# Another order of the down pairs, a longer delay before the first transposes, and a split tail, in a fused hybrid decoder layer

## The chip, the cores and the metric

The kernel runs on one core of a Trainium2 chip. The metric is the device time of one execution in microseconds. Engines are named as in the profile: PE (matmul), PEld (PE's weight loads), DVE (vector), ACT (scalar), POOL, SP (the engine whose queue issues most transfers).

## The reference

One decoder layer on 272 positions (16 meta tokens and 256 tokens), all float32. What the change touches is the feed-forward part:

```
u = rmsnorm(h, ffn_norm_w)                       # (256, 2048) matter
h = h + (silu(u @ w_gate) * (u @ w_up)) @ w_down # w_gate, w_up: (2048, 5632); w_down: (5632, 2048)
return h[:, LEAD:]                               # (256, 2048)
```

Before it stand the input projection, the attention and delta-rule heads and the output projection. They are the first 500 us or so, and the change leaves them alone.

## The kernel before

**Three matmuls for one product.** A float32 weight tile is loaded as `raw` (128 x 2 x 512, 512 KB, by SP's queue, 4 buffers), then split: ACT casts it to a rounded `hi` (L274), DVE subtracts to get `lo` (L275). Activations are kept in the same two parts. A product of 128x128 by 128x512 is then three matmuls on PE: hi by hi, hi by lo, lo by hi. In the feed-forward part there are 6 buffers for pairs of `hi` and `lo`, so splitting runs at most 6 split tiles ahead of PE.

**Chunks and blocks.** Gate and up run in 11 chunks of 512 hidden columns; the product of silu(gate) and up goes through PE transposes (`to_hT`, L1277) into `hT`, the activations of down. Chunk 0 is written by itself: `ffn_task` multiplies on DVE (L1306) and then transposes. Down runs in two blocks of 1024 output columns, `block(NCH + p, ...)` for p = 0, 1, called block 0 and block 1 here. A block goes over 22 pairs q of two k-tiles, each with two weight tiles (columns 0 to 511 and 512 to 1023 of the block).

**Plain pairs and seven pairs.** A plain pair uses its two tiles in 8 products, which is 24 matmuls. A pair listed in `DSEVEN` (7, 9, 11, 13, 15, 17, 19) is done in 7 products, 21 matmuls, by a Strassen-like scheme: both raw tiles (g, then u) have to be there, DVE forms two tiles of sums `t` and `s` by four instructions (L291 to L294), and four split tiles come of it: g, half of u, t, s. So a seven pair takes 4 of the 6 split buffers where a plain pair takes 2, and it costs DVE more and PE less. It also needs sums of the activations, made once per pair before block 0 gets there (`down_side`, `side_forms`, DVE L1318 to L1330, called side work), and the last three chunks of `hT` have to be split too (`whole`, L1466 and L1468).

**What sets the order.** The Python code is a recorder. Each `tasks.step()` between products lets side tasks emit a little work, and a `yield n` in a task makes it wait n steps. ACT's and SP's instructions stay in the order in which they were emitted; a scheduler orders PE's and DVE's when the kernel is built, and from then on every engine runs its list strictly in order. `next_w` emits the splits of tiles up to 6 ahead of the one that PE is given, and raw loads up to 3 ahead of that.

**The tail.** When a half of a block is complete, `down_end` adds it to the residual on DVE (L1516) and stores it (L1518) through SP's queue. The residual is fetched back from DRAM (`fetch_x1`, L1484) by the same queue; block 1's fetch has to wait until block 0's output has left the buffers. The last half is stored in two pieces per token block.

Of the kernel before, what the change touches and what calls it, by code (L numbers as in the profile page):

```python
# [15 lines left out]
P = 128  # L16
D = 2048
KT = D // P
# [3 lines left out]
FFN = 5632  # L22
# [3 lines left out]
NCH = FFN // 512  # L26
# [5 lines left out]
WR, WS = 4, 4  # L32
WS2 = 2
WHOLE = 8
SEVEN = (2, 4, 6)
DSEVEN = (7, 9, 11, 13, 15, 17, 19)
PER_STEP = 2
# [129 lines left out]
def layer(tc, xT, aw, x, w_in, w_ba, w_out, w_gate, w_up, w_down, cmask, dist, par, out):  # L167
    nc = tc.nc
    V, S, G, PE = nc.vector, nc.scalar, nc.gpsimd, nc.tensor
# [20 lines left out]
    tasks = Tasks(PER_STEP)  # L190
# [29 lines left out]
    wd_v = w_down.rearrange("(kt p) c -> p kt c", p=P)  # L220
    order = []
# [12 lines left out]
    def w_tile(wv, q, c):  # L234
        return wv[:, 2 * q:2 * q + 2, 512 * c:512 * (c + 1)], 2, 512
# [4 lines left out]
    forms = [("w", i) for i in range(len(order))]  # L240
    for c in range(1, NCH):
        for q in range(KT // 2):
            i = len(order)
            order += [w_tile(wv, q, c) for wv in (wg_v, wu_v)]
            forms += [("w", i), ("w", i + 1)] if q not in SEVEN else [("g", i), ("u", i), ("t", i), ("s", i)]
    for c in (0, 2):
        for q in range(FFN // P // 2):
            i = len(order)
            order += [w_tile(wd_v, q, c + j) for j in range(2)]
            forms += [("w", i), ("w", i + 1)] if q not in DSEVEN else [("g", i), ("u", i), ("t", i), ("s", i)]  # L250
    raws, ready, sums_ = {}, {}, {}

    pos = [0, 0, 0, 0]
# [127 lines left out]
    for k in range(KT):  # L381
        src, w = xr[k // 8][:, k % 8, :], aw_sb[:, k:k + 1]
# [889 lines left out]
    def to_hT(c, b, h_):  # L1272
# [7 lines left out]
        if c not in hT:  # L1280
# [3 lines left out]
            elif c < 7:  # L1284
                hT[c] = keep.tile([P, 2, 4, SEQ], F32R, tag=("v_c", "k_c", "q_c")[c - 4], name=n)
            elif c < WHOLE:
                hT[c] = fpool[0].tile([P, 2, 4, SEQ], F32R, tag=n, name=n)
            else:
                hT[c] = fpool[0].tile([P, 4, SEQ], F32, tag=n, name=n)
        bs = slice(P * b, P * (b + 1))  # L1290
        if c < WHOLE:
            S.copy(hT[c][:, 0, :, bs], pst)
# [6 lines left out]
    def ffn_task(c, b, pg, pu):  # L1299
        g_ = yield from fpool[1].get(512)  # L1300
        act(g_, pg, AF.Silu, scale=rr[:, b:b + 1])
        mm.free()
        yield at_least(f"up{c}", 1)
        yield 1
        ps = pu[b]
        V.scalar_tensor_tensor(g_, ps, rr[:, b:b + 1], g_, ALU.mult, ALU.mult)  # L1306
        mm.free()
        yield 2
        yield from to_hT(c, b, g_)


# [52 lines left out]
        yield 10  # L1364
        yield from to_hT(c, b, h_)

    def block(c, name, nq, seven, lhs, need, mid, end):

        ring, other = rings[c % 2], rings[(c + 1) % 2]
        tasks.until(lambda: ring.live == 0)  # L1370
        x = [ring.now() for _ in range(4)]
        y = []
        n = nq - len(seven)
        left = {("x", i): 3 * (2 * n + (len(seven) if i < 3 else 0)) for i in range(4)}
        left.update({("y", i): 3 * len(seven) for i in range(4)})
        todo = dict(left)

        def product(bank, a, w):
            for l, r in ((a[0], w[0]), (a[0], w[1]), (a[1], w[0])):
                first, todo[bank] = todo[bank] == left[bank], todo[bank] - 1  # L1380
                PE.matmul((x if bank[0] == "x" else y)[bank[1]], l, r, start=first, stop=todo[bank] == 0)  # L1381

        for q in range(nq):
            k = 2 * q
            if need:
                tasks.until(need(k))
            if q not in seven:
                for col in range(2):
                    hi, lo = next_w()
                    for i in range(2):  # L1390
                        for b in range(2):
                            product(("x", 2 * col + b), lhs(k + i, b), (hi[:, i], lo[:, i]))
                            tasks.step()
                    if q == nq - 1:
                        end(col, x)
                continue
            if not y:
                tasks.until(lambda: other.live == 0)
                y += [other.now() for _ in range(4)]
            tasks.until(at_least(f"side{(name, q)}", 1))  # L1400
            s1, s2_, s3, s4 = sides[name, q]
            plan = (((("y", 0), lhs(k, 0), 0), (("x", 0), lhs(k + 1, 0), 1)), ((("x", 2), s4, 1),),
                    ((("y", 3), s1, 0), (("y", 2), s3, 1)), ((("y", 1), s2_, 0), (("x", 1), lhs(k + 1, 1), 1)))
            for part in plan:
                hi, lo = next_w()
                for bank, a, i in part:
                    product(bank, a, (hi[:, i], lo[:, i]))
                    tasks.step()
            if q == seven[-1]:
                mid(y)  # L1410

    def chunk(c):
        t = []

        def end(col, x):
            if col == 0:
                for b in range(2):
                    tasks.spawn(end_task(c, b, x, t), urgent=True)

        def mid(y):  # L1420
            tasks.until(lambda: fpool[1].live == 0)
            t.extend(fpool[1].now((512,)) for _ in range(4))
            S.copy(t[0], y[0])
            tasks.spawn(mid_task(c, y, t), delay=0, urgent=True)

        block(c, "u", KT // 2, SEVEN, lhs_u, None, mid, end)
        mark(f"up{c}")

    def keep_x1():
# [16 lines left out]
    for i, q in enumerate(SEVEN):  # L1446
        k = slice(2 * q, 2 * q + 2)
# [7 lines left out]
    def whole(c):  # L1455
# [19 lines left out]
    def fetch_x1(p):  # L1475

        for j in range(2):
            n = f"hT{WHOLE + j}"
            if p == 0:
# [29 lines left out]
    def down_end(p, b, c, ps):  # L1509
        yield at_least("mid_d", p + 1)  # L1510
        parts = 1 if (p, c) != (1, 1) else 2
        w = 512 // parts
        for i in range(parts):
            cs = slice(w * i, w * (i + 1))
            r_ = x1n[p, c][:, b, cs]
            V.tensor_tensor(r_, r_, ps[:, cs], ALU.add)  # L1516
            o = 1024 * p + 512 * c + w * i
            nc.sync.dma_start(out=out[P * b:P * (b + 1), o:o + w], in_=r_)  # L1518
        rings[(NCH + p) % 2].free()

    def down_side(i, q):
# [20 lines left out]
        tasks.spawn(down_side(i, q), delay=24)  # L1542
    tasks.spawn(fetch_x1(0), delay=24)
    for p in range(2):
        def end(col, x):
            for b in range(2):
                tasks.spawn(down_end(p, b, col, x[2 * col + b]), urgent=True)

        def mid(y):
            tasks.until(lambda: fpool[1].live <= 1)  # L1550
            t = [fpool[1].now((512,)) for _ in range(3)]
            S.copy(t[0], y[0])
            tasks.spawn(down_mid(p, y, *t), delay=0, urgent=True)

        block(NCH + p, "h", FFN // P // 2, DSEVEN, lhs_h, need_h, mid, end)
        if p == 0:
            tasks.spawn(fetch_x1(1), delay=12)
    tasks.until(lambda: not tasks.list)
# [66 lines left out]
```

## Time and profile before

| | us |
|---|---|
| median of 3 runs (1222.12 to 1224.43) | 1222.2 |
| profiled execution, own time | 1224.38 |
| profiled execution, span from first to last instruction | 1222.6 |
| PE busy in the span | 1209.2 |
| DVE busy | 983.6 |
| ACT busy | 692.3 |

The clock granted to PE is full (0.9 or more) in all slices of the span. PE is busy 99% of the time, so only what makes PE stand still, and what stands before its first and behind its last matmul, can change the time unless the number of matmuls does. A busy matmul of 512 columns is shown as 0.39 us but a new one starts every 0.227 us; the matmuls overlap.

### The profile page before, as it was taken

The page shows a single profiled execution, that of the slowest core. Times are in us where ns is not written, and L with a number is a line of the kernel's source. Part 1 is how long each engine was busy: PE and PEld are TensorE (multiplying, and loading weights), DVE is VectorE, ACT ScalarE, POOL GpSimd, SP SyncE. Part 2 cuts the span into 40 slices and gives each one's busy share as a digit, 9 for nine tenths or more (in the row PEclk, how much of TensorE's full clock was granted, in tenths as well). Part 3 has the DMA queues.
Part 4 walks back from the last instruction along what each step waited for, and adds up shares of the span by engine and source line. Part 5 has one row for each costly group of instructions (what it writes and reads, how often), then busy time and mean ns, then how long its engine had stood idle before and what let it go on. Part 6 is the DMA issues. An engine that isn't in the chain of part 4 may idle for free.

```text
span 1222.6 us, 19223 instructions
## 1 busy us (share of the span) xinstructions
PE 1209.2 (99%) x7316; PEld 1060.0 (87%) x7316; DVE 983.6 (80%) x1573; ACT 692.3 (57%) x1087; POOL 6.1 (0%) x14
## 2 busy tenths in 40 slices
PE   9999999999999999999999999999999999999998
PEld 7999999999999988887888888888888888888876
DVE  7989974686676666668889988998998899886686
ACT  7674465275776665455555556555555665553552
POOL 0000000000000000000000000000000000000000
PEclk9999999999999999999999999999999999999999
DMA  8466564344544645685665665566566565567543
GB/s 293 124 207 195 145 187 121 112 124 145 172 140 139 229 162 178 191 277 167 196 206 186 195 218 190 192 204 217 166 208 216 187 211 197 201 225 276 181 164 133
DMA packets 151869, 228.54 MB, mean 187 GB/s; under 512 B 11736, under 2 KB 72672, under 8 KB 151264
## 3 DMA queue, kind: packets, MB, share of 16 engines
q1 hardware_dynamic: 151232, 226.78, 57.4%
q8 instruction: 57, 0.93, 0.3%
q10 hardware_dynamic: 544, 0.52, 0.1%
q14 instruction: 36, 0.29, 0.1%
HBM read 221.83 MB, written 5.45 MB: 186 GB/s over the span
## 4 chain that ended last, share of the span: by engine, by line
PE 85%; DVE 7%; DMA 4%; ACT 2%; issue 1%; SPq 0%; DVEq 0%; ACTq 0%
PE aux L1381 25%; PE mm L1152 23%; PE mm L1381 21%; PE mm L1199 10%; DVE lo L275 3%; DMA raw<-in_w_down_dram 3%; ACT hi L274 1%; PE aux L1100 1%; PE aux L1055 1%; DMA raw<-in_w_in_dram 0%; PE mm L1277 0%; DVE s L293 0%; DMA raw<-in_w_up_dram 0%; DVE r L581 0%; PE aux L1277 0%
## 5 line engine op out<-in xcount | busy, mean ns | idle before, releaser
L274 ACT CAST hi<-raw 128x1024 fp32r<-128x1024 f32 (+1 forms) x412 | 405.1, 996 | 325.0 <-PE mm L1152 93.3
L275 DVE TENSOR_TENSOR lo<-raw,hi 128x1024 fp32r<-128x1024 f32 (+1 forms) x412 | 470.6, 1153 | 141.6 <-ACT hi L274 139.1
L1152 PE MATMUL mm<-xh,hi 128*128 128x272 f32 (+2 forms) x896 | 258.4, 289 | 0.0
L1152 PE MATMUL mm<-xl,hi 128*128 128x272 f32 (+2 forms) x896 | 255.9, 286 | 0.9 <-DVE xl L384 0.6
L1152 PE MATMUL mm<-xh,lo 128*128 128x272 f32 (+2 forms) x896 | 255.0, 286 | 1.0 <-DVE lo L275 1.0
L1152 PEld LDWEIGHTS mm<-xl,hi 128*128 128x128 f32 x896 | 168.5, 188 | 2.2 <-DVE xl L384 2.0
L1152 PEld LDWEIGHTS mm<-xh,hi 128*128 128x128 f32 x896 | 168.6, 188 | 2.1 <-issue 1.5
L1152 PEld LDWEIGHTS mm<-xh,lo 128*128 128x128 f32 x896 | 168.2, 188 | 1.6 <-DVE lo L275 1.4
L1381 PE MATMUL aux<-hi,uh 128*128 128x512 f32 x260 | 101.6, 391 | 0.0
L1381 PE MATMUL mm<-hi,uh 128*128 128x512 f32 x260 | 101.6, 391 | 0.0
L1381 PE MATMUL aux<-hi,ul 128*128 128x512 f32 x260 | 101.3, 390 | 0.0
L1381 PE MATMUL mm<-hi,ul 128*128 128x512 f32 x260 | 101.2, 389 | 0.0
L1381 PE MATMUL aux<-lo,uh 128*128 128x512 f32 x260 | 101.2, 389 | 0.0
L1381 PE MATMUL mm<-lo,uh 128*128 128x512 f32 x260 | 101.2, 389 | 0.0
L1381 PE MATMUL aux<-hi,hT 128*128 128x512 f32 x216 | 70.2, 389 | 0.0
L1381 PE MATMUL mm<-hi,hT 128*128 128x512 f32 x216 | 70.0, 389 | 0.0
L274 ACT CAST hi<-s 128x1024 fp32r<-128x1024 f32 x44 | 46.3, 1053 | 38.0 <-DVE s L294 34.5
L291 DVE TENSOR_TENSOR t<-raw,raw 128x512 f32<-128x512 f32 x44 | 30.2, 687 | 38.7 <-DMA raw<-in_w_down_dram 25.2
L274 ACT CAST hi<-t 128x1024 fp32r<-128x1024 f32 x44 | 46.3, 1053 | 26.2 <-DVE t L292 11.3
L1381 PEld LDWEIGHTS aux<-hi,ul 128*128 128x128 f32 x260 | 48.8, 188 | 10.2
L1381 PEld LDWEIGHTS mm<-hi,ul 128*128 128x128 f32 x260 | 48.8, 188 | 10.2
L1381 PEld LDWEIGHTS mm<-hi,uh 128*128 128x128 f32 x260 | 48.8, 188 | 10.0
(418 smaller groups left out, 2046.8 us busy)
## 6 DMA issues: line engine op xcount, KB each, us to landing
raw<-in_w_in_dram SPq DMA_DIRECT2D x111, 512.0 KB, 3.6
raw<-in_w_gate_dram SPq DMA_DIRECT2D x88, 512.0 KB, 3.7
raw<-in_w_up_dram SPq DMA_DIRECT2D x88, 512.0 KB, 4.4
raw<-in_w_down_dram SPq DMA_DIRECT2D x88, 512.0 KB, 4.6
raw<-in_w_out_dram SPq DMA_DIRECT2D x32, 512.0 KB, 4.2
x<-x1d SPq DMA_DIRECT2D x8, 256.0 KB, 4.8
xr<-in_xT_dram SPq DMA_DIRECT2D x7, 272.0 KB, 5.8
out_dram<-x SPq DMA_DIRECT2D x6, 256.0 KB, 5.1
```

What stands on the lines that cost most here:

```text
L274: S.copy(hi[:, js], raw[:, js])
L275: V.tensor_tensor(lo[:, js], raw[:, js], hi[:, js], ALU.subtract)
L291: V.tensor_tensor(t[:, 0], u[:, 0], g[:, 0], ALU.subtract)
L1055: PE.matmul(pss[m][:, cut[n]], q[ms, P * n:P * (n + 1)], k[ms, 0:NK[n]], start=True, stop=True)
L1100: PE.matmul(po[:, n, :], l, r, start=(j == 0), stop=(j == 1 + n))
L1152: PE.matmul(acc[c][:, 0:n], a[:, k, cs], b[:, kt, t0:T], start=(kt == 0 and i == 0), stop=(kt == KT - 1 and i == 2))
L1199: PE.matmul(acc[b], l, r[:, i % 2, :], start=(first and i == 0 and j == 0), stop=(last and i == len(kts) - 1 and j == 2))
L1381: PE.matmul((x if bank[0] == "x" else y)[bank[1]], l, r, start=first, stop=todo[bank] == 0)
```

## The change

Four edits:

- `ROWS` sets, for each block, at which of the 22 positions a seven pair (S) or a plain pair (N) stands. The pairs of each kind keep their order. Before, pairs ran 0 to 21 in both blocks, which is `NNNNNNNSNSNSNSNSNSNSNN`.
- In `ffn_task` (chunk 0) the step count before the transposes goes from 2 to 8.
- In the last tile of block 1 PE does both products of token block 0 first, then both of token block 1 (before: alternating), and `down_end` of token block 0 is emitted between them.
- The second piece of each of the last two stores goes out through ACT's queue instead of SP's.

```
+ROWS = ("NNNNNSNSNNSNSNNSNSNSNN", "NNSNNSNNSNNSNSNSNSNNNN")
...
+    def down_rows(p):
+        plain = iter(q for q in range(FFN // P // 2) if q not in DSETS[p])
+        seven = iter(DSETS[p])
+        return [next(plain if r == "N" else seven) for r in ROWS[p]]
...
         mm.free()
-        yield 2
+        yield 8
         yield from to_hT(c, b, g_)
...
+                    last = c == NCH + 1 and col == 1 and q == rows[-1]
+                    for j in range(4):
+                        i, b = (j % 2, j // 2) if last else (j // 2, j % 2)
+                        product(("x", 2 * col + b), lhs(k + i, b), (hi[:, i], lo[:, i]))
+                        tasks.step()
+                        if last and j == 1:
+                            end(col, x, (0,))
+                    if q == rows[-1]:
+                        end(col, x, (1,) if last else (0, 1))
...
-            nc.sync.dma_start(out=out[P * b:P * (b + 1), o:o + w], in_=r_)
+            (nc.sync if i == 0 else S).dma_start(out=out[P * b:P * (b + 1), o:o + w], in_=r_)
...
-        block(NCH + p, "h", FFN // P // 2, DSEVEN, lhs_h, need_h, mid, end)
+        block(NCH + p, "h", down_rows(p), DSEVEN, lhs_h, need_h, mid, end)
```

The counts of matmuls, casts, subtractions and loads stay the same; lines move down by 8 to 13 (L275 becomes L284, L291 to L294 become L300 to L303, L1318 to L1330 become L1327 to L1339, L1468 becomes L1481, L1381 becomes L1390). In the built program PE's and DVE's lists differ from before at chunk 0's transposes and then only from block 0 on. Weight tiles of down are raw320 to raw363 in block 0 and raw364 to raw407 in block 1, two for each position.

PE at chunk 0's transposes, before (L1277 are the transposes, four matmuls each, of `gact`, which DVE's L1306 has just made):

```order
L1381 MATMUL aux_158_6787<-hi161_6674,ul_5601 128x512
L1277 MATMUL mm_69_6813<-ident_121,gact_1_6609 128x128 x4
L1381 MATMUL aux_159_6788<-hi161_6674,uh_5600 128x512
L1381 MATMUL aux_159_6788<-lo161_6675,uh_5600 128x512
L1277 MATMUL mm_70_6818<-ident_121,gact_2_6612 128x128 x4
L1381 MATMUL aux_159_6788<-hi161_6674,ul_5601 128x512
```

and now:

```order
L1390 MATMUL aux_158_6787<-hi161_6674,ul_5601 128x512
L1390 MATMUL aux_159_6788<-hi161_6674,uh_5600 128x512
L1390 MATMUL aux_159_6788<-lo161_6675,uh_5600 128x512
L1390 MATMUL aux_159_6788<-hi161_6674,ul_5601 128x512
L1390 MATMUL aux_156_6785<-hi162_6692,uh_5600 128x512
L1390 MATMUL aux_156_6785<-lo162_6693,uh_5600 128x512
L1390 MATMUL aux_156_6785<-hi162_6692,ul_5601 128x512
L1390 MATMUL aux_157_6786<-hi162_6692,uh_5600 128x512
L1390 MATMUL aux_157_6786<-lo162_6693,uh_5600 128x512
L1390 MATMUL aux_157_6786<-hi162_6692,ul_5601 128x512
L1286 MATMUL mm_69_6841<-ident_121,gact_1_6609 128x128 x4
L1286 MATMUL mm_70_6846<-ident_121,gact_2_6612 128x128 x4
```

Nine matmuls now stand ahead of the first group of transposes, and none between the two groups.

DVE in block 0, before, from the first instruction at which the lists differ in kind (L1318 to L1323: side work; lo389 to lo392: the plain tiles raw329 to raw332 of positions 4 to 6; L1468: `whole`; just ahead of it, in both lists, an L1321 on gact_52):

```order
L1318 TENSOR_TENSOR gact_53_10582<-hT5_8680 128x512
L1323 TENSOR_TENSOR gact_52_10558<-gact_51_10557,gact_52_10558 128x128
L1320 TENSOR_TENSOR gact_54_10583<-gact_53_10582 128x128
L275 TENSOR_TENSOR lo389_10484<-raw329_10420,hi389_10483 128x1024
L1321 TENSOR_TENSOR gact_54_10583<-gact_54_10583,gact_53_10582 128x128
L1322 TENSOR_TENSOR gact_54_10583<-gact_53_10582 128x128
L1323 TENSOR_TENSOR gact_54_10583<-gact_53_10582,gact_54_10583 128x128
L1318 TENSOR_TENSOR gact_55_10600<-hT6_9032 128x512
L275 TENSOR_TENSOR lo390_10502<-raw330_10438,hi390_10501 128x1024
L275 TENSOR_TENSOR lo391_10520<-raw331_10466,hi391_10519 128x1024
L1468 TENSOR_TENSOR hT_hl_10528<-hT8_9754,hT_hl_10528 128x1024
L1468 TENSOR_TENSOR hT_hl_10528<-hT9_10122,hT_hl_10528 128x1024
```

and now, from the same L1321 on (t330, s330, lo390 and lo391 belong to the first seven pair, at position 5, whose raw tiles are 330 and 331; L1327 to L1332 are the side work again):

```order
L300 TENSOR_TENSOR t330_10505<-raw331_10466,raw330_10438 128x512
L301 TENSOR_TENSOR t330_10505<-raw331_10466 128x512
L284 TENSOR_TENSOR lo389_10484<-raw329_10420,hi389_10483 128x1024
L302 TENSOR_TENSOR s330_10506<-raw331_10466,t330_10505 128x512
L1332 TENSOR_TENSOR gact_52_10564<-gact_51_10563,gact_52_10564 128x128
L303 TENSOR_TENSOR s330_10506<-raw330_10438,s330_10506 128x512
L284 TENSOR_TENSOR lo390_10502<-raw330_10438,hi390_10501 128x1024
L1327 TENSOR_TENSOR gact_53_10586<-hT5_8680 128x512
L1329 TENSOR_TENSOR gact_54_10587<-gact_53_10586 128x128
L1331 TENSOR_TENSOR gact_54_10587<-gact_53_10586 128x128
L1330 TENSOR_TENSOR gact_54_10587<-gact_54_10587,gact_53_10586 128x128
L284 TENSOR_TENSOR lo391_10524<-raw331_10466,hi391_10523 128x512
```

The seven pair's four instructions for the sums have moved in among the side work. Before, raw332's subtraction (lo392) is 13 instructions behind that L1321. Now it is lo394, 42 instructions stand in between, and this is where it comes, behind the side work for the pairs 7 to 15 and `whole`:

```order
L1327 TENSOR_TENSOR gact_59_10644<-hT_hl_10534 128x512
L1339 TENSOR_TENSOR rest_10389<-gact_58_10621,rest_10389 128x384
L1329 TENSOR_TENSOR gact_60_10645<-gact_59_10644 128x128
L1331 TENSOR_TENSOR gact_60_10645<-gact_59_10644 128x128
L1330 TENSOR_TENSOR gact_60_10645<-gact_60_10645,gact_59_10644 128x128
L284 TENSOR_TENSOR lo394_10652<-raw332_10487,hi394_10651 128x1024
L1332 TENSOR_TENSOR gact_60_10645<-gact_59_10644,gact_60_10645 128x128
```

Behind it come 12 more instructions, two of them for the sums of the next seven pair, and then lo395 (raw333, the other tile of position 6). The split of a tile is emitted when PE is given the tile six split buffers ahead, and the four of a seven pair use these up, so ACT's cast for raw332 has gone behind the side work's casts in the same way.

PE at position 6 of block 0 now (tile 395 is raw333, the second tile of the plain pair; tile 396 is raw334, g of the next seven pair):

```order
L1390 MATMUL aux_207_10391<-hi394_10651,hT2_7588 128x512
L1390 MATMUL aux_208_10392<-hi395_10694,hT2_7588 128x512
L1390 MATMUL aux_209_10393<-hi395_10694,hT2_7588 128x512
L1390 MATMUL mm_121_10690<-hi396_10706,hT4_8310 128x512
L1390 MATMUL aux_206_10390<-hi396_10706,hT4_8310 128x512
L1390 MATMUL aux_208_10392<-lo395_10695,hT2_7588 128x512
L1390 MATMUL aux_208_10392<-hi395_10694,hT2_7588 128x512
```

Four matmuls that use only a `hi` stand ahead of the first that uses lo395. Nowhere else in down, before or now, does a later tile stand ahead of an earlier one; before, PE's rows there read like any other plain tile:

```order
L1381 MATMUL aux_207_10391<-hi392_10564,hT3_7952 128x512
L1381 MATMUL aux_208_10392<-hi393_10607,hT3_7952 128x512
L1381 MATMUL aux_208_10392<-lo393_10608,hT3_7952 128x512
L1381 MATMUL aux_208_10392<-hi393_10607,hT3_7952 128x512
L1381 MATMUL aux_209_10393<-hi393_10607,hT3_7952 128x512
L1381 MATMUL aux_209_10393<-lo393_10608,hT3_7952 128x512
```

DVE in block 1 at a seven pair that follows one plain pair, before (position 19, raw tiles 402 for g and 403 for u; lo487 and raw401 are the second tile of the plain pair ahead of it):

```order
L275 TENSOR_TENSOR lo486_12067<-raw400_12005,hi486_12066 128x1024
L291 TENSOR_TENSOR t402_12100<-raw403_12070,raw402_12032 128x512
L292 TENSOR_TENSOR t402_12100<-raw403_12070 128x512
L293 TENSOR_TENSOR s402_12101<-raw403_12070,t402_12100 128x512
L275 TENSOR_TENSOR lo487_12085<-raw401_12030,hi487_12084 128x1024
L294 TENSOR_TENSOR s402_12101<-raw402_12032,s402_12101 128x512
L275 TENSOR_TENSOR lo488_12097<-raw402_12032,hi488_12096 128x1024
L275 TENSOR_TENSOR lo489_12110<-raw403_12070,hi489_12109 128x512
```

and now at the third seven pair of block 1 (position 8, raw tiles 380 and 381), which follows two plain pairs:

```order
L284 TENSOR_TENSOR lo456_11621<-raw378_11544,hi456_11620 128x1024
L284 TENSOR_TENSOR lo457_11630<-raw379_11594,hi457_11629 128x1024
L284 TENSOR_TENSOR lo458_11642<-raw380_11612,hi458_11641 128x1024
L300 TENSOR_TENSOR t380_11645<-raw381_11624,raw380_11612 128x512
L301 TENSOR_TENSOR t380_11645<-raw381_11624 128x512
L302 TENSOR_TENSOR s380_11646<-raw381_11624,t380_11645 128x512
L284 TENSOR_TENSOR lo459_11658<-raw381_11624,hi459_11657 128x512
L303 TENSOR_TENSOR s380_11646<-raw380_11612,s380_11646 128x512
```

Before, the subtraction for the tile that PE needs first (lo487) stood behind three instructions that need the seven pair's u. Now at positions 2, 5, 8 and 11 the tiles of the plain pairs and g stand ahead of them; at 13, 15 and 17 sums stand ahead of plain tiles as before. In block 0 that is so at 5, 7, 17 and 19 now.

On SP's queue block 0's fetch of the residual (x1, four transfers) has moved ahead of raw336, behind which it was, and block 1's ahead of raw373 and raw374. The last two stores of 128 x 256 for column half 1 are one for each token block on SP now, and one for each on ACT.

More of the change, by code (lines that the diff above doesn't have):

```diff
@@ L245, in layer @@
             forms += [("w", i), ("w", i + 1)] if q not in SEVEN else [("g", i), ("u", i), ("t", i), ("s", i)]
-    for c in (0, 2):
-        for q in range(FFN // P // 2):
+    DSETS = (DSEVEN, DSEVEN + ())
+    def down_rows(p):
+        plain = iter(q for q in range(FFN // P // 2) if q not in DSETS[p])
+        seven = iter(DSETS[p])
+        return [next(plain if r == "N" else seven) for r in ROWS[p]]
+    for p in range(2):
+        for q in down_rows(p):
             i = len(order)
-            order += [w_tile(wd_v, q, c + j) for j in range(2)]
-            forms += [("w", i), ("w", i + 1)] if q not in DSEVEN else [("g", i), ("u", i), ("t", i), ("s", i)]
+            order += [w_tile(wd_v, q, 2 * p + j) for j in range(2)]
+            forms += [("w", i), ("w", i + 1)] if q not in DSETS[p] else [("g", i), ("u", i), ("t", i), ("s", i)]
     raws, ready, sums_ = {}, {}, {}
@@ L1365, in end_task, with block @@
         yield from to_hT(c, b, h_)
-    def block(c, name, nq, seven, lhs, need, mid, end):
+    def block(c, name, rows, seven, lhs, need, mid, end):
         ring, other = rings[c % 2], rings[(c + 1) % 2]
@@ L1372, in block @@
         y = []
-        n = nq - len(seven)
+        n = len(rows) - len(seven)
         left = {("x", i): 3 * (2 * n + (len(seven) if i < 3 else 0)) for i in range(4)}
@@ L1381, in product @@
                 PE.matmul((x if bank[0] == "x" else y)[bank[1]], l, r, start=first, stop=todo[bank] == 0)
-        for q in range(nq):
+        for q in rows:
             k = 2 * q
@@ L1389, in block @@
                     hi, lo = next_w()
[L1390 to L1395, printed above, removed]
+                    last = c == NCH + 1 and col == 1 and q == rows[-1]
[7 more added lines that the diff above has]
+                        end(col, x, (1,) if last else (0, 1))
                 continue
@@ L1413, in chunk, with end @@
         t = []
-        def end(col, x):
+        def end(col, x, blocks):
             if col == 0:
-                for b in range(2):
+                for b in blocks:
                     tasks.spawn(end_task(c, b, x, t), urgent=True)
@@ L1424, in mid @@
             tasks.spawn(mid_task(c, y, t), delay=0, urgent=True)
-        block(c, "u", KT // 2, SEVEN, lhs_u, None, mid, end)
+        block(c, "u", range(KT // 2), SEVEN, lhs_u, None, mid, end)
         mark(f"up{c}")
@@ L1544, in layer, with end @@
     for p in range(2):
-        def end(col, x):
-            for b in range(2):
+        def end(col, x, blocks):
+            for b in blocks:
                 tasks.spawn(down_end(p, b, col, x[2 * col + b]), urgent=True)
```

## The prediction

> **What bounds the kernel now.** I read the windows by stage first, then PE's waits, then the chain of waits around the longest of them. The windows are the stretch before down, block 0, block 1, and what follows the last matmul. Columns: length, then busy time (instructions) of PE, PEld, DVE, ACT, POOL, then granted clock, DMA share, GB/s.
>
> ```profile
> 983.40:1099.30 115.90, 115.90 (x517) 96.04 (x516) 107.26 (x154) 66.56 (x81) 0.00 (x0) 1.00 0.61 206
> 1099.30:1218.40 119.10, 115.82 (x507) 94.55 (x505) 85.67 (x99) 52.70 (x54) 0.00 (x0) 1.00 0.56 190
> 1218.40:1222.60 4.20, 0.00 (x0) 0.00 (x0) 0.76 (x3) 0.00 (x0) 0.00 (x0) 1.00 0.37 125
> 983.40:1022.30 38.90, 38.90 (x178) 32.27 (x177) 38.00 (x76) 21.13 (x33) 0.00 (x0) 1.00 0.57 190
> ```
>
> Block 0 is bound by PE without a gap, but DVE works 107.3 of its 115.9 us, and 38.0 of the first 38.9. Block 1 has PE idle for 3.3 us although DVE has much room. The waits of PE that the change can reach are two groups, one in block 1 and one at chunk 0's transposes (total, times, longest):
>
> ```profile
> PE mm L1381 <- DVE lo L275: 3.3, 3, 1.8
> PE mm L1277 <- DVE gact L1306: 1.3, 1, 1.3
> ```
>
> From the chain of waits (start, length, what): how fast matmuls follow each other, then the starts of the last five seven pairs of block 1 (L291 is the first instruction of the sums), and the last of them with what stands around it.
>
> ```profile
> 956.91 6.12 PE mm L1381 x27
> ...
> 1150.09 0.69 DVE t L291
> ...
> 1161.23 0.69 DVE t L291
> ...
> 1173.09 0.69 DVE t L291
> ...
> 1184.55 0.69 DVE t L291
> ...
> 1189.95 6.77 DMA raw<-in_w_down_dram
> ...
> 1196.84 0.69 DVE t L291
> ...
> 1198.74 1.15 DVE lo L275
> ...
> 1199.93 2.81 PE mm L1381 x11
> ```
>
> A matmul costs 6.12 / 27 = 0.2267 us. A plain pair is then 5.44 us of PE, a seven pair 4.76, one of each 10.20. The seven pairs start 11.1, 11.9, 11.5 and 12.3 us apart, so the supply loses 1 to 2 us on each round. The last round shows how: u is issued when its buffer comes free, takes 6.8 us to land, the sums start, and the plain tile's lo, which needs no u, is done only 3.05 us later (1199.89 against 1196.84) because it stands behind three of their instructions. PE takes it at 1199.93.
>
> **Chunk 0, 2 steps to 8.** Timeline at the wait:
>
> ```profile
> 562.36 0.39 PE L1381 MATMUL aux<-hi,ul 128*128 128x512 f32 x1
> ...
> 563.29 0.74 DVE L1306 SCALAR_TENSOR_TENSOR gact<-mm,rr,gact 128x512 f32<-128x512 f32 x1
> ...
> 564.08 0.66 PE L1277 MATMUL mm<-ident,gact 128*128 128x128 f32 x4 [1.34 <-DVE gact L1306]
> 564.15 0.74 DVE L1306 SCALAR_TENSOR_TENSOR gact<-mm,rr,gact 128x512 f32<-128x512 f32 x1
> ```
>
> From one start to the next are 1.72 us instead of 0.23, so 1.5 us are lost. Nine more matmuls (2.04 us) now run in that time, so the transposes come at 564.6, behind the first L1306 (ends 564.03); their second group comes at 565.1, behind the second (564.89). Gain 1.5 us, covered by 0.2 to 0.6 us of margin; without it the loss would be what is missing, at most the old 1.5.
>
> **Block 0, the term that goes the other way.** The first seven pair stands two positions earlier, in the stretch where DVE has 0.9 us free. DVE's rows there:
>
> ```profile
> 996.07 0.28 DVE L1321 TENSOR_TENSOR gact<-gact,gact 128x128 f32<-128x128 f32 x1
> ...
> 1002.92 2.35 DVE L1468 TENSOR_TENSOR hT_hl<-hT,hT_hl 128x1024 fp32r<-128x1024 f32 x2
> 1005.19 1.22 DVE L1468 TENSOR_TENSOR rest<-hT,rest 128x1024 fp32r<-128x1024 f32 x1
> 1006.33 1.22 DVE L275 TENSOR_TENSOR lo<-raw,hi 128x1024 fp32r<-128x1024 f32 x1
> ...
> 1012.63 0.28 DVE L1321 TENSOR_TENSOR gact<-gact,gact 128x128 f32<-128x128 f32 x1
> 1012.83 0.55 DVE L1330 TENSOR_TENSOR side<-gact,side 128x384 fp32r<-128x384 f32 x1
> 1013.30 0.28 DVE L1323 TENSOR_TENSOR gact<-gact,gact 128x128 f32<-128x128 f32 x1
> ...
> 1016.72 0.68 DVE L291 TENSOR_TENSOR t<-raw,raw 128x512 f32<-128x512 f32 x1
> 1017.32 0.68 DVE L292 TENSOR_TENSOR t<-raw 128x512 f32<-128x512 f32 x1
> ```
>
> By starts, a 128x1024 subtraction costs 1.14 us (1005.19 to 1006.33), a 128x512 one 0.60, a 128x384 one 0.47, a 128x128 one 0.20. From the common L1321, done at 996.27, the new list holds up to and with lo394 (raw332): 8 x 1.14 + 9 x 0.60 + 5 x 0.47 + 21 x 0.20 = 21.1 us. Its first instruction needs u (raw331):
>
> ```profile
> 992.31 0.37 SPq L261 DMA_DIRECT2D raw<-in_w_down_dram  x1
> ...
> raw<-in_w_down_dram SPq DMA_DIRECT2D x3, 512.0 KB, 5.1
> ...
> 1022.25 0.39 PE L1381 MATMUL mm<-hi,hT 128*128 128x512 f32 x1
> ```
>
> It was issued at 992.31; the three loads around it have a median of 5.1 us, so it lands at 997.4, and a little later behind its neighbour; I take 998.1. Then lo394 is done at 1019.2. PE began the first seven pair at 1022.25 after seven plain ones; after five it is 1022.25 - 48 x 0.2267 = 1011.4, and position 6 comes 21 matmuls later at 1016.1. PE waits there 2.8 us. Up to lo395 DVE has 1 x 1.14 + 3 x 0.60 + 2 x 0.47 + 7 x 0.20 = 5.3 us more, until 1024.5. PE's list gives it the rest of tile 394 and four hi matmuls first, nominally until 1016.1 + 16 x 0.2267 = 1019.8. So the two waits cost 4.7 us in all. After that the seven pair at 7 has its t and s 0.5 us before PE wants them, and two plain pairs let DVE catch up. Bounds: 3.0 if u had landed by 996.3, 5.7 if DVE also stands 0.9 us for ACT as in the old stretch. I take 4.7, since the landing is nearest to a row. What is late next is nothing: PE's delay gives every later tile the same time.
>
> [...]
>
> **Block 1.** 507 matmuls at 0.2267 are 114.9 us; the stretch took 119.1, so 4.2 us are lost, the waits and the restarts. Before, the sums at positions 11, 13, 15 and 17 started 7.7, 6.7, 5.1 and 3.8 us ahead of PE's arrival without waits (1099.3 plus the PE time of the pairs ahead). PE needs the second plain tile 2.72 us before the seven pair and its lo comes 3.05 after the start, so the lead has to be 5.8 us; the waits begin where it falls below that. A round took 11.5 us: 5.4 from the sums' start until u's buffer is free (3 halves, a lo, a half, a lo, half a lo by the costs above) and 6.1 to land.
>
> Now the rounds at the front have two plain pairs, 15.64 us of PE, so the supply is ahead again at 5, 8 and 11, and 11 starts with the same 7.7 us, since PE's freeing of split buffers and not DVE sets it there. From 11 to 13 a round costs 3.0 + 6.1 = 9.1 us, because lo of u now stands right behind the third sum; from 13 to 15 6.4 + 6.1 = 12.5, with two plain tiles among the sums; from 15 to 17 11.5 as before. Against 10.20 of PE the leads are 8.8, 6.5 and 5.2 at 13, 15 and 17. That is 0.6 us short at one place. Positions 17 and 19 of block 0 have the same pattern, and there the plain tile has about 1 us to spare. I put 0.6 us for all of it (bounds 0 and 4, the second being the old loss in one block, or half of it in both). Gain 4.2 - 0.6 = 3.6.
>
> What SP's queue is moved past: block 0's fetch now precedes raw336, which waits for raw332's split anyway. In block 1 the fetch waits for the output to land:
>
> ```profile
> 1107.42 4.26 SPq L1484 DMA_DIRECT2D x<-x1d  x4
> 1111.74 90.87 SPq L261 DMA_DIRECT2D raw<-in_w_down_dram  x33
> ```
>
> So raw373, which was out before the fetch, leaves at about 1111.7. With 6.8 us to land and 2.3 for hi and lo it is ready at 1120.8; PE needs it 105 matmuls into block 1, at 1123.1. Hidden with 2 us to spare; beyond that each us costs one.
>
> **The tail.** The last additions and stores (durations min/median/max in ns and first and last start in the fourth row; the fifth is of the kernel's first loads, the only ones from ACT's queue before):
>
> ```profile
> 1217.99 0.39 PE L1381 MATMUL mm<-hi,rest 128*128 128x512 f32 x1
> ...
> 1218.75 0.41 DVE L1516 TENSOR_TENSOR x<-x,mm 128x256 f32<-128x256 f32 x1
> ...
> 1219.09 0.89 SPq L1518 DMA_DIRECT2D out_dram<-x  x2
> ...
> L1518 SPq DMA_DIRECT2D out_dram<-x x10: 332/357/432, 1101.6 to 1219.6; - x10
> ...
> L261 ACTq DMA_DIRECT2D raw<-in_w_in_dram x2: 463/476/488, 0.7 to 1.2; - x2
> ```
>
> The last two additions still wait for the last matmul and end at 1219.16. SP issued the last store from 1219.6 to 1219.98, behind its sister. ACT's queue is idle and can start at 1219.2; its issue takes 0.48 us instead of 0.36. Gain 0.4 - 0.1 = 0.3 us; bounds a loss of 0.1 (ACT starts no earlier than SP did) and a gain of 0.9 (both issues of the pair off the end). Token block 0's earlier additions are hidden already.
>
> **Sum.** -1.5 - 3.6 + 4.7 - 0.3 = -0.7 us: span 1221.9 instead of 1222.6, and the profiled execution's own 1224.4 us would be 1223.7. That execution was 2.2 above the median of the runs; on the median of 1222.2 it is 1221.5.
>
> **Rivals.** (1) Block 0 hides the earlier seven pair: DVE starts the sums at once, or the side work runs ahead. Then 1222.2 - 1.5 - 3.6 - 0.3 = 1216.8. For it speaks that raw332's old lo stood at 1006.33, 9 us ahead of PE; against it, that each of the 43 instructions has a price from a row and DVE takes them in order. (2) Slower: in block 0 as well as in block 1 the last single plain pairs fall below the 5.8 us of lead, because a u takes 7 us instead of 6.1 (the row above has 6.8, a slower one costs each round the difference). The place is the plain pairs ahead of positions 17 and 19 in block 0, 15 and 17 in block 1; it decides when the lead there has fallen by 1.5 us. Each block then loses about 2 us, half of the old 4.2: 1222.2 - 1.5 - 4.2 + 4 + 4.7 - 0.3 = 1224.9. (3) The order does nothing in block 1, so the old 4.2 stay: 1225.1; against it, that three of six rounds are gone.
>
> **How the numbers follow.** Below 0.2% (2.4 us) a measurement of this kernel tells little from no change, by the spread of 2.3 us of the three runs. My forecast, waits of 3 to 5.7 us in block 0 with a small rest elsewhere, has 0.58 and gives 1219.5 to 1223; rival 1 and what lies between has 0.27, rivals 2 and 3 together 0.15. Faster is rival 1 and a part of the low end of the forecast: 0.30; slower is rivals 2 and 3 less what stays within the bound: 0.12; same 0.58. The range reaches to rival 1 and near to rival 2: 1216.5 to 1224.7.
>
> **What would show it.** Right: PE's wait for L1306 gone; at position 6 of block 0 two waits of PE for lo (L284), about 2.8 and 1.9 us; block 1 with less than 1 us of them; the first seven pair's L300 just ahead of side work at about 996 to 997 (all is 1.5 earlier); last store on ACT's queue. Wrong, if block 0's window shows PE without a gap (then 1216.8), or if waits appear at positions 15 to 19 of block 0.

## The result, and the profile after

The changed kernel took 1226.46 us (median of 9 runs) against 1222.96 us for the kernel before: ratio 1.0028, 95% interval [1.0015, 1.0042]. Measured again beside other runs it stood at 1.0015 [1.0003, 1.0028]. By these two figures the change costs 1.8 to 3.4 us, where 1221.5 us and a range up to 1224.7 had been forecast. The profiled execution took 1229.4 us, the slowest of the nine, with a span of 1227.6.

The windows of the kernel after, by the same stages as before (the columns as there: length, busy time of PE, PEld, DVE, ACT, POOL, then granted clock, DMA share, GB/s), and its waits of PE in down:

```profile
984.30:1104.60 120.30, 118.35 (x517) 96.85 (x516) 106.44 (x152) 67.51 (x81) 0.00 (x0) 0.99 0.60 199
1104.60:1223.70 119.10, 116.19 (x507) 94.48 (x506) 86.58 (x100) 52.46 (x54) 0.00 (x0) 1.00 0.57 190
1223.70:1227.60 3.90, 0.00 (x0) 0.00 (x0) 0.75 (x2) 0.00 (x0) 0.00 (x0) 1.00 0.40 132
```

```profile
PE mm L1390 <- DVE lo L284: 2.4, 2, 1.4
PE aux L1390 <- DVE lo L284: 1.4, 2, 1.0
PE aux L1390 <- ACT hi L283: 0.9, 1, 0.9
```

Block 0 (with what little stands ahead of it) grew from 115.9 to 120.3 us. Block 1 has exactly its old 119.1, although its order is new: the old waits are replaced by others, not removed. From the last matmul's end to the end of the span are 3.9 us instead of 4.2. The wait for L1306's product at chunk 0 is gone.

From here on "lost" means what a position of a block took beyond its matmuls at 0.2267 us each. The kernel before lost 0 in block 0 and 4.2 in block 1, the changed one 4.4 and 4.2. With 1.5 gained at chunk 0 and 0.3 at the tail that is +2.6 us in these two traces. Their spans differ by 5.0 us; the other 2.4 stand ahead of down, most of it one wait of 2.0 us at 152 us, far ahead of the first instruction whose order was changed. Block 0's part lies where it was forecast. The first fence is DVE around it, the second PE (the brackets hold the idle time and what ended it), the third the granted clock behind the waits:

```profile
998.25 0.69 DVE L300 TENSOR_TENSOR t<-raw,raw 128x512 f32<-128x512 f32 x1 [0.98 <-DMA raw<-in_w_down_dram]
...
1011.17 0.68 DVE L1327 TENSOR_TENSOR gact<-hT 128x512 f32<-128x512 f32 x1
...
1014.39 0.68 DVE L1327 TENSOR_TENSOR gact<-hT 128x512 f32<-128x512 f32 x1
...
1016.67 0.68 DVE L1327 TENSOR_TENSOR gact<-hT_hl 128x512 f32<-128x512 f32 x1
...
1018.35 1.21 DVE L284 TENSOR_TENSOR lo<-raw,hi 128x1024 fp32r<-128x1024 f32 x1
...
1019.68 0.68 DVE L1327 TENSOR_TENSOR gact<-hT_hl 128x512 f32<-128x512 f32 x1
```

```profile
1018.09 0.50 PE L1390 MATMUL aux<-hi,hT 128*128 128x512 f32 x1 [0.93 <-ACT hi L283]
...
1019.62 0.50 PE L1390 MATMUL aux<-lo,hT 128*128 128x512 f32 x1 [1.02 <-DVE lo L284]
```

```profile
1019.62:1021.12 1.50, 1.50 (x5) 1.19 (x6) 1.50 (x7) 0.81 (x2) 0.00 (x0) 0.82 0.14 46
1021.12:1022.83 1.71, 1.71 (x6) 1.32 (x5) 1.71 (x6) 0.95 (x2) 0.00 (x0) 0.50 0.82 266
1022.83:1024.06 1.23, 1.23 (x4) 0.95 (x3) 1.23 (x3) 1.23 (x2) 0.00 (x0) 0.53 0.00 0
```

Each L1327 row is the start of one seven pair's side work (L1318 in the kernel before). The four shown belong to the last four seven pairs, which PE reaches at position 12 and later; they stand ahead of or right behind lo394, which PE waits for at 1019.6. PE first waits for hi394, because ACT's cast stands behind casts of the side work. Behind the waits PE runs at half clock for 3.4 us, which is 1.6 us of matmuls lost.

In block 1 of the changed kernel the waits have moved to positions 4, 5, 14 and 16. From its chain of waits:

```profile
1106.94 0.60 DVE t L300
...
1108.74 0.60 DVE x L1529
...
1112.34 0.72 DVE lo L284
1113.06 6.64 DMA out_dram<-x
...
1120.62 0.38 SPq L270
1121.10 6.50 DMA raw<-in_w_down_dram
1127.70 1.06 ACT hi L283
1128.79 1.22 DVE lo L284
...
1171.62 7.61 DMA raw<-in_w_down_dram
1179.36 0.69 DVE t L300
```

The sums of block 1's first seven pair (1106.94) stand between the last additions of block 0, so the last of its stores leaves 8.7 us into block 1 instead of 5.4. The fetch of x for block 1 waits for them to land, and raw373 and raw374 stand behind it on SP's queue until 1120.6. PE waits for these two at positions 4 and 5 (1.2 us) and again at 14 and 16 (3.0 us).

### The profile page after: what moved, and what is told of

Read it like the earlier page. It is cut to its first block, busy times and chain, and to the rows that moved or that the text cites. A ratio compares the mean times of both kernels' runs of the same rounds, so it can differ in the third digit from the quotient of the medians.

```text
span 1227.6 us, 19219 instructions
## 1 busy us (share of the span) xinstructions
PE 1212.5 (99%) x7316; PEld 1060.9 (86%) x7316; DVE 983.9 (80%) x1573; ACT 692.1 (56%) x1087; POOL 6.0 (0%) x14
## 4 chain that ended last, share of the span: by engine, by line
PE 68%; DVE 17%; DMA 9%; ACT 3%; issue 3%; SPq 0%; DVEq 0%; ACTq 0%
PE mm L1161 18%; PE mm L1390 17%; PE aux L1390 16%; PE mm L1208 11%; DVE lo L284 8%; DMA raw<-in_w_down_dram 6%; ACT hi L283 2%; DVE r L590 1%; DVE s L302 1%; DMA raw<-in_w_up_dram 1%; DMA raw<-in_w_in_dram 1%; PE aux L1109 1%; DVE t L301 1%; DVE s L303 1%; DVE t L300 1%
## 5 line engine op out<-in xcount | busy, mean ns | idle before, releaser
L284 DVE TENSOR_TENSOR lo<-raw,hi 128x1024 fp32r<-128x1024 f32 (+1 forms) x412 | 470.6, 1154 | 148.0 <-ACT hi L283 145.3
L1390 PE MATMUL aux<-hi,uh 128*128 128x512 f32 x260 | 101.6, 391 | 0.0
L1390 PE MATMUL mm<-hi,uh 128*128 128x512 f32 x260 | 101.6, 391 | 0.0
L1390 PE MATMUL aux<-hi,ul 128*128 128x512 f32 x260 | 101.2, 389 | 0.0
L1390 PE MATMUL mm<-hi,ul 128*128 128x512 f32 x260 | 101.2, 389 | 0.0
L1390 PE MATMUL mm<-lo,uh 128*128 128x512 f32 x260 | 101.2, 389 | 0.0
L1390 PE MATMUL aux<-lo,uh 128*128 128x512 f32 x260 | 101.2, 389 | 0.0
L1390 PE MATMUL aux<-hi,hT 128*128 128x512 f32 x216 | 71.7, 397 | 0.9 <-ACT hi L283 0.9
L1390 PE MATMUL mm<-hi,hT 128*128 128x512 f32 x216 | 70.2, 390 | 0.0
L1390 PEld LDWEIGHTS aux<-hi,ul 128*128 128x128 f32 x260 | 48.8, 188 | 10.2
L1390 PEld LDWEIGHTS mm<-hi,ul 128*128 128x128 f32 x260 | 48.8, 188 | 10.1
L1390 PEld LDWEIGHTS aux<-hi,uh 128*128 128x128 f32 x260 | 48.8, 188 | 10.0
L1390 PEld LDWEIGHTS mm<-lo,uh 128*128 128x128 f32 x260 | 48.8, 188 | 10.0
```

What stands on the lines that cost most here:

```text
L284: V.tensor_tensor(lo[:, js], raw[:, js], hi[:, js], ALU.subtract)
```

## The experiments

All are edits of the changed kernel except the first, which is one of the kernel before. "Ratio" is to the kernel before, with its 95% interval.

**Each part by itself.**

The pause alone:

```diff
-        yield 2
+        yield 8
         yield from to_hT(c, b, g_)
```

> The kernel before with only chunk 0's pause made 8 steps. Theory: PE's 1.5 us gap at the first transposes of chunk 0 goes and nothing else moves, so 1.5 us faster than before, about 1221.5 us. Rival: the pause moves later work of chunk 0 into another gap (a gap of 0.5 us and a matmul at 0.25 instead of 0.23 us stand near 653 us in the changed kernel), so the gain is 1 us or less.

Measured: ratio 0.9993 [0.9983, 1.0004], 1223.6 us. The gap at chunk 0 is gone, all eight transposes follow each other at 565.1, and no other gap of its size came up. The interval holds both expectations. Its profiled execution (1220.1 us, the fastest of its 12) lost only 1.0 us in block 1 with the old order there, where the profile of before had 4.2: that loss is no constant of the order.

Block 0 in the old order:

```diff
-ROWS = ("NNNNNSNSNNSNSNNSNSNSNN", "NNSNNSNNSNNSNSNSNSNNNN")
+ROWS = ("NNNNNNNSNSNSNSNSNSNSNN", "NNSNNSNNSNNSNSNSNSNNNN")
```

> The changed kernel with block 0 of down in its old order. Theory: the 4.4 us lost in block 0 (two gaps of PE, 2.4 us, and nine matmuls at half clock, 2.0 us) are all due to block 0's order, so it is 4.4 us faster than the changed kernel, about 1222.0 us, with PE without a gap in block 0 and the granted clock at 1.00 throughout; block 1 still loses 4 us. Rival: the waits in block 1 come from what block 0's delay did to the loads; then they go as well and it is 7 to 8 us faster, about 1219 us.

Measured: ratio 0.9963 [0.9952, 0.9975], 1219.7 us. The rival won: with block 0's order the waits in block 1 went too. Block 0 and block 1 in its windows:

```profile
984.60:1100.50 115.90, 115.90 (x517) 96.06 (x516) 108.09 (x155) 66.56 (x81) 0.00 (x0) 1.00 0.63 209
1100.50:1215.40 114.90, 114.88 (x507) 94.78 (x505) 85.56 (x98) 52.67 (x54) 0.00 (x0) 1.00 0.59 197
```

Block 1 takes the 114.9 us of its matmuls and nothing more. So the new order of block 1 does what the prediction said in this trace, where block 0 is left alone.

Block 1 in the old order (the second string replaced by "NNNNNNNSNSNSNSNSNSNSNN"):

> The changed kernel with block 1 of down in its old order. Theory: the new order of block 1 gains nothing, since its waits of 4.0 us stand against 4.2 us before; so the time is that of the changed kernel within 0.5 us, about 1226.5 us, the output of block 0 is stored within 4 us of block 0's end, and block 0 shows its two gaps and the half clock again. Rival (the prediction's): the new order is worth 3.6 us, and the time is 1230 us. If the half clock depends on where the gaps fall in time, block 0's loss may be 2 us smaller in this run.

Measured: ratio 1.0063 [1.0051, 1.0075], 1232.1 us, the slowest of all. Here the rival was nearer, and even it was too low: by the ratios this version is 4.3 to 5.9 us above the two measurements of the changed kernel. The old order loses 5.6 us in block 1 behind the new block 0. Block 0 lost 5.3, with longer gaps than in the changed kernel, yet at full clock:

```profile
1019.57:1021.10 1.53, 0.51 (x2) 0.19 (x2) 1.53 (x4) 0.26 (x1) 0.00 (x0) 1.00 0.00 0
1021.10:1023.49 2.39, 2.39 (x10) 1.98 (x11) 2.39 (x10) 0.95 (x3) 0.00 (x0) 1.00 0.48 148
1023.49:1024.87 1.38, 0.39 (x2) 0.00 (x0) 1.38 (x4) 1.38 (x3) 0.00 (x0) 1.00 0.32 123
```

At full clock PE arrives early at the second tile and waits 1.15 us for it; at half clock it doesn't. Position 6 lost 3.34 us here and 3.32 in the changed kernel. The half clock cost nothing, because the second tile sets the end either way.

The tail as before:

```diff
-                    last = c == NCH + 1 and col == 1 and q == rows[-1]
+                    last = False
...
-            (nc.sync if i == 0 else S).dma_start(out=out[P * b:P * (b + 1), o:o + w], in_=r_)
+            nc.sync.dma_start(out=out[P * b:P * (b + 1), o:o + w], in_=r_)
```

> The changed kernel with its last tile used as before and all stores on SP's queue. Theory: the tail is worth 0.3 us, so about 1226.8 us, with 4.6 us from the last matmul's start to the end of the span instead of 4.3. Rival: the other order of the last tile brings nothing, and the store queues alone or neither make the difference: the same 4.3 us. Block 0 is as in the changed kernel, and shows whether its half clock comes back in another execution.

Measured: ratio 1.0034 [1.0022, 1.0046], 1228.2 us, and 4.5 us from the last matmul's start to the end of the span, against 4.6 before and 4.3 in the changed kernel. The tail is worth 0.2 to 0.3 us by the traces; the times alone don't resolve it. This version takes both edits of the tail back, so it doesn't tell the order of the last tile from the store queues. Block 0 lost 5.2 us, again with the half clock.

**Why block 1 depends on block 0.**

Block 0's first seven pair at position 6:

```diff
-ROWS = ("NNNNNSNSNNSNSNNSNSNSNN", ...
+ROWS = ("NNNNNNSNSNSNSNNSNSNSNN", ...
```

> The changed kernel with block 0's first seven pair at position 6 instead of 5 and the next two one position earlier or later, so that its last three stand where the changed kernel has them (15, 17, 19). Theory H, handed on: block 0's waits and the double plain pair ahead of 15 make the sums of its last seven pair start 1.6 us nearer to PE's arrival, and block 1's early seven pairs turn that into waits. Then PE has 5.4 us more in block 0 and waits there less than 0.5 us, the clock stays at 1.00, and block 1 loses between 0 and 4 us by the lead of the seven pair at 19: 8.2 us of it gives no wait, 6.6 us gives 4. Time 1219.7 to 1223.7 on the scale on which the kernel before is 1224.3. Rival, each block by itself: block 1 loses 4 us unless block 0 has the old order, 1223.7.

Measured: ratio 1.0013 [1.0002, 1.0024], 1225.9 us. The part on block 0 was a miss: it still lost 5.3 us, again with the half clock, since the later seven pair finds its own casts behind the same side work: ACT's cast of s stands behind casts of side work that wait for DVE. The longest wait:

```profile
PE mm L1390 <- ACT hi L283: 2.3, 1, 2.3
```

The lead, which is the time from the start of a seven pair's sums to PE's arrival at it, was 6.7 us at position 19 of block 0, and block 1 lost 2.5 us.

Block 0 with plain pairs at its end:

```diff
-ROWS = ("NNNNNSNSNNSNSNNSNSNSNN", ...
+ROWS = ("NNNNNSNNSNSNSNSNSNSNNN", ...
```

> The changed kernel with block 0's first seven pair still at position 5, but no double plain pair behind position 7 and three plain pairs at its end instead of two. Theory H: the waits of 4.4 to 5.2 us at positions 5 and 6 stay, but the last seven pair ends early, block 1 starts with as much lead as with the old order, and its waits go: 4.5 to 5 us above the run with block 0's old order (1219.7), so about 1224.5. Rival, the wait itself delays the loads for good: block 1 still loses 4 us, about 1228.

Measured: ratio 1.0012 [1.0000, 1.0024], 1225.2 us. Block 0 lost 4.7 us (again without the half clock), block 1 only 1.0. So the wait in block 0 isn't what block 1 suffers from. What changed is the lead that block 0 hands over (7.1 us instead of 6.6), and with it raw373 leaves earlier (15.3 us into block 1 instead of 16.2).

The fetch late:

```diff
-            tasks.spawn(fetch_x1(1), delay=12)
+            tasks.spawn(fetch_x1(1), delay=60)
```

> The changed kernel with the fetch of x for block 1 emitted 60 steps after block 0 instead of 12, so that no load of block 1 stands behind it on SP's queue. Theory F, the fetch: it holds raw373 back from 1113.8 until 1120.6, from which the waits at positions 4 and 5 come (1.2 us), and the lead is short from there on, so all 4 us of block 1 go and the time is 4 us below the changed kernel, about 1224. Theory H: the 1.2 us at positions 4 and 5 go, those at 14 and 16 (3.0 us) stay for the most part, since the u of the seven pair at 15 still leaves 6.65 us after the sums ahead of it: about 1227.

Measured: ratio 1.0018 [1.0006, 1.0030], 1225.9 us. In its trace theory F holds: block 1 lost 0.2 us, at 14 and 16 too, with block 0's 4.3 unchanged. SP's queue and block 1's window:

```profile
1112.88 0.93 SPq L1531 DMA_DIRECT2D out_dram<-x  x2
1113.91 28.28 SPq L270 DMA_DIRECT2D raw<-in_w_down_dram  x13
1142.24 1.99 SPq L1497 DMA_DIRECT2D x<-x1d  x4
```

```profile
1104.50:1219.60 115.10, 115.05 (x507) 94.73 (x505) 88.00 (x101) 52.67 (x54) 0.00 (x0) 1.00 0.60 197
```

The loads now follow the stores at once. The times don't show this gain: 1.0018 lies between the changed kernel's 1.0015 and 1.0028, and the time is some 2 us above what the two losses give (table below). 1.7 us of it stand at 154 us in its profile, far ahead of the change; whether that is the rest in its other executions can't be seen from one trace.

The pause back at 2, with block 0 in the old order:

```diff
-        yield 8
+        yield 2
```

> The changed kernel with block 0 in its old order and chunk 0's pause at 2 steps again. Theory: only PE's gap of 1.5 us at chunk 0's transposes comes back, so 1.5 us above the run with block 0's old order alone, about 1221.2 us where that had 1219.7. Rival: the pause is worth nothing in the whole, since the time gained at chunk 0 is waited for later: 1219.7. Block 1 is again without a wait in both.

Measured: ratio 0.9982 [0.9968, 0.9996], 1221.3 us: 1.9 thousandths or 2.3 us above the run without it, with overlapping intervals. The gap is back, 1.2 us in this trace, and block 1 lost 1.0, so "without a wait in both" was a miss.

**What makes block 0's wait, and versions without it.**

The side work of the last four seven pairs later:

```diff
-        tasks.spawn(down_side(i, q), delay=24)
+        tasks.spawn(down_side(i, q), delay=24 if i < 3 else 20 * i - 16)
```

> The changed kernel with the side work of the last four seven pairs of down emitted later (44, 64, 84 and 104 steps after the start of block 0 instead of 24 for all). Theory S, the side work: in the changed kernel DVE does the side work of pairs that PE needs 30 us later ahead of the lo that PE waits for at positions 5 and 6; some 5.4 us of it then stands behind the first lo and 3 us more behind the second, so both come before PE does: block 0 loses less than 0.5 us instead of 4.4 to 5.2, and the granted clock stays at 1.00. Block 1 loses what the fetch costs, 1 to 4 us. So 4 to 6 us below the changed kernel of this call. Rival, the loads: raw332 to raw335 or the free buffers bind, and the waits at positions 5 and 6 stay above 3 us.

Measured: ratio 1.0009 [0.9997, 1.0020], 1224.9 us. The waits at positions 5 and 6 are gone, PE has no gap in the whole stretch, and the clock is 1.00:

```profile
1008.00:1026.00 18.00, 18.00 (x81) 14.91 (x80) 17.87 (x29) 8.65 (x14) 0.00 (x0) 1.00 0.60 198
```

So it is the early side work, and not the loads, that made lo394 late. The gain was smaller than expected, 1.5 us by the times: block 0 lost 0.2 us at position 8 and 1.3 at 18, and block 1 still 3.7. At 18 it is no side work: DVE itself stood idle for the u of that round, which had not landed.

```profile
1081.74 0.69 DVE L300 TENSOR_TENSOR t<-raw,raw 128x512 f32<-128x512 f32 x1 [3.68 <-DMA raw<-in_w_down_dram]
```

The same with the fetch late:

> The same with the fetch for block 1 late as well (60 steps instead of 12). Theory S with the fetch: neither block has a wait of PE over 0.5 us, 8 us below the changed kernel of this call and 4.5 us below the kernel before. Rival: the late side work of block 0 takes DVE time that the later seven pairs of block 0 need, so that waits of 1 us or more come up behind position 10.

Measured: ratio 1.0000 [0.9988, 1.0012], 1224.1 us. Block 1 lost 0.4 us, block 0 3.2: the rival's mechanism at position 8 (1.6 us, with the deferred side work in front of the lo again), earlier than the rival had placed it, and a late u at 18 (1.6 us).

Block 0's old order with the fetch late:

> The changed kernel with block 0 in its old order and the fetch late. Theory: block 0 has no wait; the rest of block 1's (0 in one execution of the old order with the early fetch, 1.6 us in another) is below 0.3 us: 5 us below the kernel before and 0.5 to 1 us below the run with the old order alone. Rival: the fetch costs nothing where the lead is there, and the time is the same as with the old order alone.

Measured: ratio 0.9963 [0.9949, 0.9977], 1219.5 us, and no loss in either block. The late fetch adds nothing that the times show where the lead is there. This version and the one with block 0's old order alone are the fastest, about 4.5 us below the kernel before.

The changed kernel again:

> The changed kernel itself, on the chip of these three, so that they are compared at one place: 3.4 us above the kernel before by the first measurement. In its profile the waits at positions 5 and 6 of block 0 come to 4.4 to 5.3 us together, whether the clock halves or not; block 1 loses 1 to 4 us, more where the u of the seven pair at 15 takes over 7 us to land.

Measured: 1.0015 [1.0003, 1.0028], 1226.5 us. Block 0 lost 4.1 us with the half clock, block 1 3.6 at positions 4, 5, 14 and 16.

The losses of all versions beside the measured times, with the two things that sort them. "Lead" is from the start of the sums of block 0's last seven pair to PE's arrival at it; "raw373" is when it leaves SP's queue, from the start of block 1; the last column is (ratio - 1) x 1223 us.

```
version                       block 0  block 1  lead  raw373  time
before                          0.0      4.2     6.7    5.8     0
before, pause 8                 0.0      1.0     8.9    4.2   -0.9
block 1 old                     5.3      5.6     6.1    8.2   +7.7
changed                         4.4      4.2     6.6   16.2   +3.4
changed, again                  4.1      3.6     5.7   16.6   +1.8
tail old                        5.2      3.5     5.7   15.9   +4.2
side work later                 1.5      3.7     5.7   16.5   +1.1
first seven at 6                5.3      2.5     6.7   15.8   +1.6
plain end                       4.7      1.0     7.1   15.3   +1.5
block 0 old, pause 2            0.0      1.0     7.8   15.5   -2.2
block 0 old                     0.0      0.0     8.2   14.4   -4.5
fetch late                      4.3      0.2     6.4    9.6   +2.2
side work and fetch later       3.2      0.4     5.8    9.6    0.0
block 0 old, fetch late         0.0      0.0     8.5    8.4   -4.5
```

With block 1's new order and the early fetch, the loss in block 1 falls from about 4 to 0 as the lead rises from 6 to 8 us. It falls as regularly with the time of raw373, and these versions don't part the two. With the late fetch the leads are as short (6.4 and 5.8 us) and the loss is 0.2 and 0.4. So in this order a short lead by itself costs little; the loads held behind the fetch cost it, and the lead goes with how late they are. By the prediction's figures raw373 may leave up to 14.7 us into the block (PE needs it after 23.8, and landing, hi and lo take 9.1): the versions in which it leaves later lose 1.0 us or more, the others at most 0.4. In block 1's old order raw373 leaves ahead of the fetch and long before PE needs it, and the three traces go by the lead: 5.6 us lost at 6.1, 4.2 at 6.7, 1.0 at 8.9.

Counting from -4.5 for the two versions without loss, the losses (with chunk 0's gap of 1.2 to 1.5 us and the tail's 0.3 where they stand) come within 2.3 us of every measured time. That is as much as many of the differences between versions. Each loss is read from one execution and each time from several, and in the twelve traces with the pause at 8, whose PE lists agree up to block 0, block 0's first product starts anywhere from 981.8 to 985.8 us. So it is the traces that part the causes; the times bear out the gain with block 0's old order, but not the 4.0 us that the late fetch gains in its trace.

## Why the prediction was right or wrong

Three of the four terms of the sum came out: -1.5 at chunk 0, +4.4 for +4.7 in block 0, -0.3 at the tail. The fourth, -3.6 for block 1, was 0.0 in the changed kernel.

- **Chunk 0, -1.5.** Right in the trace: the wait is gone, at no cost. By times 2.3 us with block 0 in the old order and 0.9 on the kernel before, both with intervals that hold 1.5.
- **Block 0, +4.7.** Right in size and place: 4.1 to 5.3 us at positions 5 and 6 in the five traces with this order and the early side work. Lo394 was done at 1019.56 (forecast 1019.2 on the scale of before, where PE was 0.9 us earlier). Two details were off: the first wait is shared between ACT's hi and DVE's lo, and in four of the five traces the second shows as half clock (0.50) instead of a wait.
- **"What is late next is nothing: PE's delay gives every later tile the same time."** This step failed. For waits of PE inside block 0 it nearly held: behind position 6 no position of those five traces lost over 0.15 us, and position 19 had 5.7 to 6.6 us of lead against the 5.7 at which PE waits. But block 1 starts from what DVE has left to do at the end of block 0. The lead at position 19 was 5.7 to 6.6 us in the five traces with this order and the early side work, and 6.7 to 8.9 in the five with the old order. PE's delay is not the reason, since the version with plain pairs at the end has the same delay and loses only 1.0 us in block 1.
- **Block 1, -3.6.** Right for the order by itself: with block 0's old order two traces have no loss in block 1 and a third 1.0 us. The forecast lead of 7.7 us at position 11 (counted from 1099.3; by the measure used here it was 7.5 before) was 8.2 in the version with block 0's old order, and at 13, 15 and 17 the leads were 10.1, 7.4 and 6.5 against 8.8, 6.5 and 5.2; PE waits where the lead falls to 5.7, as worked out (5.8). In the changed kernel position 11 had 6.6 and the gain was 0. With the fetch late it had 7.7 and 7.5 in spite of the short lead at the end of block 0, so the sentence that 11 "starts with the same 7.7 us" holds where the loads aren't held back. The size of the term was read from one execution: the old order's 4.2 us stood in a run 2.2 above the median. By the times block 1's order with block 0's old one is worth 1.9 us (both with the pause at 2), 2.7 (from the version with block 0 old, less chunk 0 and tail) or 3.3 (both with the pause at 8).
- **SP's queue, "hidden with 2 us to spare".** This term was mis-sized, and through it block 1's gain was lost. That raw373 comes behind the fetch was seen, but not that the sums of a seven pair at position 2 go ahead of block 0's last additions and so of the stores, nor that block 0's order makes these additions later. The last of the stores left 5.4 us into block 1 before, 7.8 with either order alone new and 8.7 with both (9.4 in the second trace of the changed kernel). Raw373 left at 16.2 us where the estimate had 12.6 and 14.7 was the limit. The missing 1.5 us cost 1.2 at positions 4 and 5, and in all 4.2, where "each us costs one" had been said. With the fetch late, the traces have 0.2 and 0.4 of it left.
- **Tail, -0.3.** Right: 4.6 to 4.3 us. An issue on ACT's queue took 0.36 us there, not the 0.48 taken from the first loads.
- **The rivals.** The result went the way of (3), block 1 keeps its 4.2 and 1225.1, but the old waits didn't stay, as (3) has it: they went, and new ones came for want of lead, which is nearer to (2). (2) had put it down to a slow u and given block 1 and block 0 2 us each. Both had 0.15 together; the sum has no term by which block 0's order acts on block 1.
- **The clock.** The sum has no term for it. Behind the waits in block 0 the granted clock was 0.50 for 3.4 us, after idle stretches of PE of 0.9 and 1.0 us. The 1.6 us of matmuls lost there cost nothing: position 6 lost 3.32 us here and 3.34 at full clock in the version with block 1's old order.

## What to carry to other kernels

Price two reorderings of neighbouring stages together: what one leaves over is the lead in us that it hands to the next, measured at the last tile of the stage and set against the lead with which the next begins to wait. Before a tile is moved to the front of a stage, look at what the previous stage still has in the queues of DVE and SP, above all at stores that a later load has to follow. A loss read from one profiled execution can be several times that of another (4.2 and 1.0 us here for one order of down), so a gain is not to be set at the whole of it.

## What the runs showed of the hardware

The granted clock was at half behind some gaps of PE and at full behind others. In the changed kernel, both times, and in the versions with the old tail and the late fetch, two gaps of 0.7 to 1.8 us and of 1.3 us (lost time), 2.5 to 3.5 us from the start of the first to the end of the second, were followed by 3.4 us at 0.50. The version with block 0's first seven pair at 6 shows 3.4 us of it behind gaps of 2.5, 0.4 and 0.3 us. The same pair of gaps at 1.9 and 1.3 us, and at 1.6 and 1.3, left it at 1.00 in the versions with the old block 1 and the plain end. A single gap of 2.0 us at 152 us in the changed kernel left it at 1.00 as well, in the gap and behind it:

```profile
152.42:154.68 2.26, 0.27 (x3) 0.04 (x2) 2.26 (x6) 1.75 (x3) 0.00 (x0) 1.00 1.07 361
154.68:158.00 3.32, 3.32 (x86) 3.29 (x87) 3.32 (x12) 2.68 (x10) 0.00 (x0) 1.00 0.92 257
```

In the changed kernel a matmul ran between the two gaps, at 1018.09, and PE stood idle for 0.93 us ahead of it and 1.02 us behind it. Why the same pair of gaps halves the clock in one execution and not in another is not shown.

One and the same burst of four loads, issued at the same spacing (2.5, 1.1 and 0.6 us), the loads for the seven pair at position 15 of block 1, landed its last one 6.1 us after issue with block 0's old order and 7.6 in the changed kernel. That makes 1.5 of the 3.0 us by which the sums at 15 come later against PE's matmuls there (1.7 us less lead, and the 1.3 us that PE waits at 14). By itself it doesn't make PE wait: with block 0's old order and the fetch late it took 7.5 us, and nothing was lost. The cause of the difference stays open.
